# Hybrid decoder trunk: the activations become the loaded operand and the weights move past them, 512 columns a product; outputs by token, turned between stages

## The chip, the cores and the metric

The kernel runs on one core of a Trainium2 chip. It is judged by the device time of the whole program in microseconds, as the median of several runs. The engines spoken of are TensorE (PE in the rows, its loads of the stationary operand PEld), VectorE (DVE), ScalarE (ACT), GpSimd (POOL) and SyncE (SP), which issues the loads.

## The reference, cut to what matters

Two layers over 256 tokens of 1024 channels, all float32:

```python
for l in range(DEPTH):
    h = rms_norm(x, ffn1_norm[l])
    x = x + 0.5 * swiglu_ffn(h, ffn1_w_gate[l], ffn1_w_up[l], ffn1_w_down[l])   # 1024 -> 2816 -> 1024
    h = rms_norm(x, mix_norm[l])
    p = h @ w_in[l]                                                             # 1024 -> 2176
    a_val, a_gate, b_u, b_v, c_b, c_c, c_x = jnp.split(p, SPLITS, axis=-1)
    a = a_val * jax.nn.sigmoid(a_gate)
    a = causal_depthwise_conv(a, conv_a_w[l]) + conv_a_b[l]                     # width 31, 384 channels
    a = jax.nn.silu(layer_norm(a, ln_a_g[l], ln_a_b[l]))
    b = chunked_spatial_gating(jax.nn.gelu(b_u), jax.nn.gelu(b_v), ...)
    c = c_b * causal_depthwise_conv(c_c * c_x, conv_c_w[l])                     # width 3
    x = x + jnp.concatenate([a, b, c], axis=-1) @ w_out[l]
    h = rms_norm(x, ffn2_norm[l])
    x = x + 0.5 * swiglu_ffn(h, ffn2_w_gate[l], ffn2_w_up[l], ffn2_w_down[l])
return rms_norm(x, final_norm)
```

## The kernel before, in words

Everything lies by channel: x is eight tiles of 128 channels x 256 tokens. A weight matrix is cut in blocks of 128x128; a block is the stationary operand of TensorE and the 256 tokens move past it. The 2544 blocks of the whole program come from HBM in the order in which they are used, 8 blocks (512 KB) to a page, 318 pages.

Products are made in three parts. Each page is split in two fp32r pages, `hi` by a cast on ACT (L128) and `lo` = raw - hi on DVE (L129); activations are split in the same way and lie as hi|lo, 512 columns, side by side. `mm` (L170) makes a block's product with two matmuls: `wh` past all 512 columns (L175), then `wl` past the 256 hi columns (L176). So a finished bank holds two halves, and `whole` (L178) adds them with an ACT copy and a DVE add. Pages are split ahead of their use (`split_to`, `weights`, up to AHEAD = 14 pages); in the mixer `state["cap"]` stops that at the end of the mixer's own weights. A few products are made in plain float32 from the raw pages, one matmul call to a block that the chip runs as two instructions (`mm_native`, L149): the first 16 blocks of the program, and 40 blocks of each `w_out`.

A feed-forward part runs in two halves: gate and up projections of 11 column blocks, SiLU, split, then the down projection of that half, which is added to x. A norm's scale is a number per token, that is per column here: the squares are summed by small matmuls (`token_sums`, L270), the root is made on DVE (`rsqrt_rows`, L236), and the result is spread over the partitions by two small matmuls (L260).

The mixer's projections come in the order of `IN_ORDER`: group A first (gate and value of three channel blocks), then B, then C. As soon as a block of A has its gate and value, its convolution of 31 taps is queued in `back`: 16 products by ACT (L446, L449), the other 15 taps and the sums by DVE (L458, L451, L460, L461). `drain(BACK)` puts three of the queued steps behind each projection, and the rest after the last one. The mean of the layer norm over A (`m_la_mean`, L417) needs all three convolutions, and the products of `w_out` with A's channels come last in its order.

TensorE, DVE and ACT run their instructions in the order that the program's scheduler wrote, which follows the code above with small shifts; page splits of ACT and DVE stand in that same order.

Of the kernel before, what the change touches and what calls it, by code (L numbers as in the profile page):

```python
# [8 lines left out]
F32 = mybir.dt.float32  # L9
# [39 lines left out]
C_B = 2 * NA + 2 * NB
C_C, C_X = C_B + NC, C_B + 2 * NC  # L50
IN_ORDER = [t for i in range(NA) for t in (A_GATE + i, A_VAL + i)]
IN_ORDER += [B_V + i for i in range(NB)] + [B_U + i for i in range(NB)]
IN_ORDER += [t for i in range(NC) for t in (C_C + i, C_X + i, C_B + i)]

PAGE_BLOCKS = 8
PAGE = PAGE_BLOCKS * P
RAWS = 6
PARTS = 15
LOAD_AHEAD = 6
AHEAD = 14  # L60
PACE = 1.6
NEXT = 4
WORK = 12
EVAC = 6
WARM = 8
HALF = FT // 2
STEPS = 3
AFTER = 2
N_OPEN = 5
NATIVE_OUT = 5  # L70
WIDE = 16
BACK = 3
OUT = (2, 2, 2, 2)
# [3 lines left out]
def hybrid_trunk(ctx, tc, x_t, par, w_st, b_s, wts, out):  # L77
# [5 lines left out]
    work = ctx.enter_context(tc.tile_pool(name="work", bufs=WORK))  # L83
    tmp = ctx.enter_context(tc.tile_pool(name="tmp", bufs=2))
    ps_mm = ctx.enter_context(tc.tile_pool(name="ps_mm", bufs=6, space=PSUM))
    ps_sm = ctx.enter_context(tc.tile_pool(name="ps_sm", bufs=2, space=PSUM))

    spare = []

    def single(name):  # L90

        if not spare:
            pair = work.tile([P, 2, T], F32, tag="w", name=f"{name}_2")
            spare.extend([pair[:, 1, :], pair[:, 0, :]])
        return spare.pop()
# [15 lines left out]
    state = {"at": 0, "cap": None, "credit": 0.0}  # L111
# [20 lines left out]
    def native(n):  # L132

        at = state["at"]
        state["at"] += n
        last = (at + n - 1) // PAGE_BLOCKS
        load_to(last + LOAD_AHEAD)
        got = []
        for i in range(at, at + n):
            raw = loaded[i // PAGE_BLOCKS]  # L140
            c = i % PAGE_BLOCKS * P
            got.append(raw[:, c:c + P])
        while len(pages) <= last:
            pages.append(None)
        return got

    def mm_native(ps, w, act, ks, first, last):
        for k in ks:
            nc.tensor.matmul(ps, w[k], act[k], start=k == first, stop=k == last)  # L149

    def weights(n, ahead=True):
# [11 lines left out]
        got = []  # L163
        for i in range(at, at + n):
            hi, lo = pages[i // PAGE_BLOCKS]
            c = i % PAGE_BLOCKS * P
            got.append((hi[:, c:c + P], lo[:, c:c + P]))
        return got

    def mm(ps, w, act, ks, first, last):  # L170


        for k in ks:
# [4 lines left out]
    def whole(ps, name):  # L178

        if len(ps.shape) == 2:  # L180
            return ps
        lo = tmp.tile([P, T], F32, tag="e", bufs=EVAC, name=f"{name}_lo")
        nc.scalar.copy(lo, ps[:, 1, :])  # L183
        sm = tmp.tile([P, T], F32, tag="e", bufs=EVAC, name=f"{name}_sm")
        nc.vector.tensor_add(sm, ps[:, 0, :], lo)  # L185
        return sm
# [5 lines left out]
    ps = ps_sm.tile([P, P], F32, tag="sm", name="warm")  # L192
    for _ in range(WARM):
        nc.tensor.matmul(ps, ones_sq, ones_sq, start=True, stop=True)
    x_sb = acts.tile([P, DT, T], F32, tag="x", name="x_sb")
    x = [x_sb[:, d, :] for d in range(DT)]
    xall = x_t.rearrange("p (d t) -> p d t", t=T)
    par_sb = const.tile([P, NCOLS], F32, name="par_sb")
    nc.sync.dma_start(par_sb, par)
    for i in range(2):  # L200
        raw = raws.tile([P, PAGE], F32, tag="raw", name=f"raw{i}")
        loaded.append(raw)
    Q, H = DT // 4, PAGE // 2
    for n, (i, h) in enumerate(((0, 0), (1, 0), (0, 1), (1, 1))):
        nc.sync.dma_start(x_sb[:, n * Q:(n + 1) * Q, :], xall[:, n * Q:(n + 1) * Q, :])
        nc.sync.dma_start(loaded[i][:, h * H:(h + 1) * H], wts[i][:, h * H:(h + 1) * H])
# [5 lines left out]
    bsb = const.tile([P, NB, CHUNK], F32, name="bsb")  # L212

    apad = [const.tile([P, WA - 1 + T], F32, name=f"apad{i}") for i in range(NA)]
    zpad = [const.tile([P, WC - 1 + T], F32, name=f"zpad{i}") for i in range(NC)]
    for t, n in [(t, WA - 1) for t in apad] + [(t, WC - 1) for t in zpad]:
        nc.gpsimd.memset(t[:, :n], 0.0)

    def load_gating(l):
        nc.sync.dma_start(wst, w_st[l])  # L220
        nc.sync.dma_start(bsb, b_s[l])

# [5 lines left out]
    def col(l, name, i):  # L228
        c = (L * LCOLS if name == "final_norm" else l * LCOLS + COL[name]) + i
        return par_sb[:, c:c + 1]  # L230

    def pin(ins):
        return tc.keep_in_program_order(ins)


    def rsqrt_rows(ps, scale, eps, name, between=None):  # L236

        m = tmp.tile([P, 2], F32, tag="rs_m", name=f"{name}_m")
        nc.vector.tensor_scalar(m, ps, scale, eps, ALU.mult, ALU.add)
# [16 lines left out]
        if between is not None:  # L256
            between()
# [8 lines left out]
    def token_sums(tiles, name):  # L266
        ps = ps_sm.tile([P, 2], F32, tag="sm", name=f"{name}_ps")
        for h in range(2):
            for n, t in enumerate(tiles):
                pin(nc.tensor.matmul(  # L270
                    ps[:, h:h + 1], t[:, h * P:(h + 1) * P], ones,
                    start=n == 0, stop=n == len(tiles) - 1,
                ))
        return ps

    class Norm:


        def __init__(self, l, name):
            self.l, self.name, self.act = l, name, {}  # L280
            self.id = f"{name}{l}"
            self.sums = []
            self.first = False

        def begin(self):

            self.first, self.scaled = True, []
            for d in range(DT):
                xg = single(f"{self.id}_xg{d}")
                nc.vector.tensor_scalar(xg, x[d], col(self.l, self.name, d), None, ALU.mult)  # L290
                self.scaled.append(xg)
                x2 = acts.tile([P, 2, T], F32R, tag=f"x2{d}", name=f"{self.id}_x2{d}")
                nc.scalar.copy(x2[:, 0, :], xg)
                nc.vector.tensor_sub(x2[:, 1, :], xg, x2[:, 0, :])
                self.act[d] = x2

        def feed(self, d, split=True):
            if split:
                g = col(self.l, self.name, d)
                x2 = acts.tile([P, 2, T], F32R, tag=f"x2{d}", name=f"{self.id}_x2{d}")  # L300
                nc.scalar.activation(x2[:, 0, :], x[d], AF.Copy, scale=g)
                nc.vector.scalar_tensor_tensor(  # L302
                    x2[:, 1, :], x[d], g, x2[:, 0, :], ALU.mult, ALU.subtract)
                self.act[d] = x2
            self.square(d)
            if not split:
                nc.scalar.activation(x[d], x[d], AF.Copy, scale=col(self.l, self.name, d))
# [423 lines left out]
```

## Time and profile before

| | |
|---|---|
| time, median of 3 runs | 963.05 us (962.9 to 967.27) |
| the profiled execution | 961.55 us, its span 959.8 us |
| mean granted TensorE clock, share of full speed | 0.985 |
| busy share of the span: PE, DVE, ACT | 97%, 81%, 59% |

The span runs from the first to the last instruction that the profiler saw; 1.75 us of the profiled execution lie outside it. Times in rows are microseconds from the span's start.

### The profile page before, as it was taken

The numbers are of one execution on the slowest core, as the hardware profiler recorded it, in microseconds if no ns is written. First come the engines' busy times: TensorE is split into PE (matmuls) and PEld (weight loads), VectorE is DVE, ScalarE is ACT, GpSimd is POOL, SyncE is SP. The second block draws the span as 40 slices with busy tenths as digits, with TensorE's granted clock in tenths as the row PEclk, the third lists the DMA queues.
The fourth block names the chain that finished last, engine by engine and source line by source line (L and its number), as shares of the span: only waits on it lengthen the run. The fifth ranks groups of instructions, "written<-read, shape, count | busy, mean of one in ns | idle before, by whom it ended". The sixth has DMA issues, their size and how long they took to land.

```text
span 959.8 us, 14578 instructions
## 1 busy us (share of the span) xinstructions
PE 934.6 (97%) x5280; PEld 812.6 (85%) x5280; DVE 776.9 (81%) x1456; ACT 568.7 (59%) x1052; POOL 3.0 (0%) x14
## 2 busy tenths in 40 slices
PE   9999999999979999999999999999997999999995
PEld 7888888888868888888888888888886888888885
DVE  6998777878969997777987777778987799878733
ACT  6875555578257864555655545556952677645522
POOL 0000000000000000000000000000000000000000
PEclk9999999999979999999999999999998999999998
DMA  8995555530037975555555555554300789555101
GB/s 297 320 347 192 185 194 188 186 133 22 17 114 261 340 272 184 190 195 181 189 181 186 187 190 186 195 184 145 111 1 0 245 284 341 196 188 194 45 1 44
DMA packets 48024, 170.70 MB, mean 178 GB/s; under 512 B 5328, under 2 KB 5712, under 8 KB 47952
## 3 DMA queue, kind: packets, MB, share of 16 engines
q1 hardware_dynamic: 47952, 169.77, 50.8%
q8 instruction: 41, 0.67, 0.3%
q14 instruction: 31, 0.25, 0.1%
HBM read 168.71 MB, written 1.05 MB: 177 GB/s over the span
## 4 chain that ended last, share of the span: by engine, by line
PE 91%; DVE 6%; DMA 2%; ACT 1%; issue 0%; DVEq 0%; SPq 0%
PE f_pd L175 17%; PE f_pu L175 17%; PE f_pg L175 17%; PE f_pd L176 9%; PE f_pu L176 8%; PE f_pg L176 8%; PE m_p L175 7%; PE m_p L176 4%; PE m_po L149 1%; DMA raw<-wts 1%; DVE m_ac_acc L458 1%; DVE lo L129 1%; DVE m_ac_acc L451 1%; PE f_pg L149 1%; DMA x_sb<-x_t 0%
## 5 line engine op out<-in xcount | busy, mean ns | idle before, releaser
L129 DVE TENSOR_TENSOR lo<-raw,hi 128x1024 fp32r<-128x1024 f32 x306 | 371.8, 1222 | 95.3 <-ACT hi L128 93.8
L128 ACT CAST hi<-raw 128x1024 fp32r<-128x1024 f32 x306 | 318.8, 1051 | 212.8 <-PE f_pd L175 71.6
L175 PE MATMUL f_pg<-ffn_norm_x,hi 128*128 128x512 f32 x696 | 247.4, 395 | 1.7 <-DVE ffn_norm_x L302 1.7
L175 PE MATMUL f_pd<-f_m,hi 128*128 128x512 f32 x704 | 247.2, 396 | 0.0
L175 PE MATMUL f_pu<-ffn_norm_x,hi 128*128 128x512 f32 x696 | 247.0, 394 | 0.0
L176 PE MATMUL f_pd<-f_m,lo 128*128 128x256 f32 x704 | 195.5, 280 | 0.0
L176 PE MATMUL f_pg<-ffn_norm_x,lo 128*128 128x256 f32 x696 | 194.4, 279 | 0.0
L176 PE MATMUL f_pu<-ffn_norm_x,lo 128*128 128x256 f32 x696 | 194.3, 279 | 0.0
L175 PEld LDWEIGHTS f_pd<-f_m,hi 128*128 128x128 f32 x704 | 131.9, 188 | 32.1 <-DVE f_m L334 1.4
L175 PEld LDWEIGHTS f_pg<-ffn_norm_x,hi 128*128 128x128 f32 x696 | 130.5, 187 | 32.3 <-DVE ffn_norm_x L302 2.3
L175 PEld LDWEIGHTS f_pu<-ffn_norm_x,hi 128*128 128x128 f32 x696 | 130.5, 187 | 30.0
L176 PEld LDWEIGHTS f_pd<-f_m,lo 128*128 128x128 f32 x704 | 132.8, 189 | 0.5
L176 PEld LDWEIGHTS f_pg<-ffn_norm_x,lo 128*128 128x128 f32 x696 | 131.2, 188 | 0.3 <-DVE lo L129 0.3
L176 PEld LDWEIGHTS f_pu<-ffn_norm_x,lo 128*128 128x128 f32 x696 | 131.2, 188 | 0.1
L175 PE MATMUL m_p<-mix_norm_x,hi 128*128 128x512 f32 x304 | 108.1, 398 | 0.0
L176 PE MATMUL m_p<-mix_norm_x,lo 128*128 128x256 f32 x304 | 85.9, 283 | 0.0
L175 PEld LDWEIGHTS m_p<-mix_norm_x,hi 128*128 128x128 f32 x304 | 57.1, 188 | 12.9
L176 PEld LDWEIGHTS m_p<-mix_norm_x,lo 128*128 128x128 f32 x304 | 57.4, 189 | 0.4 <-issue 0.2
L389 ACT ACTIVATE f_sg<-f_g 128x256 f32<-128x256 f32 x88 | 36.4, 414 | 17.5 <-DVE f_g L387 17.3
L185 DVE TENSOR_TENSOR f_wd_sm<-f_pd,f_wd_lo 128x256 f32<-128x256 f32 x64 | 26.8, 419 | 20.6 <-ACT f_wd_lo L183 20.6
L333 ACT CAST f_m<-f_m 128x256 fp32r<-128x256 f32 x88 | 35.4, 402 | 10.5 <-DVE f_m L391 7.2
L458 DVE SCALAR_TENSOR_TENSOR m_ac_acc<-apad,par_sb,m_ac_acc 128x256 f32<-128x256 f32 x90 | 40.8, 481 | 0.8 <-ACT m_ac_acc L446 0.7
(242 smaller groups left out, 843.2 us busy)
## 6 DMA issues: line engine op xcount, KB each, us to landing
raw<-wts SPq DMA_DIRECT2D x316, 512.0 KB, 4.3
x_sb<-x_t SPq DMA_DIRECT2D x4, 256.0 KB, 5.2
raw<-wts SPq DMA_DIRECT2D x4, 256.0 KB, 5.4
out<-x_sb SPq DMA_DIRECT2D x4, 256.0 KB, 2.4
wst<-w_st SPq DMA_DIRECT2D x2, 256.0 KB, 4.3
bsb<-b_s SPq DMA_DIRECT2D x2, 128.0 KB, 4.2
par_sb<-par SPq DMA_DIRECT2D x1, 143.0 KB, 2.3
```

Of the source, the lines that this page charges most:

```text
L128: nc.scalar.copy(hi, loaded[i])
L129: after(nc.vector.tensor_sub(lo, loaded[i], hi), held[0])
L149: nc.tensor.matmul(ps, w[k], act[k], start=k == first, stop=k == last)
L175: nc.tensor.matmul(ps, wh, x2, start=k == first, stop=False)
L176: nc.tensor.matmul(ps[:, 0, :], wl, x2[:, 0, :], start=False, stop=k == last)
L185: nc.vector.tensor_add(sm, ps[:, 0, :], lo)
L333: nc.scalar.copy(x2[:, 0, :], src)
L389: nc.scalar.activation(sg, g, AF.Silu)
L451: nc.vector.tensor_add(acc, acc, t)
L458: yield lambda j=j: nc.vector.scalar_tensor_tensor(acc[:, j % 4, :], ap[:, j:j + T], wt[j], acc[:, j % 4, :], ALU.mult, ALU.add)
```

## The change

The operands of TensorE change places. An activation tile of 128 channels x 128 tokens is loaded (`xh` or `xl`), and 512 columns of a weight page move past it, so an output has 128 tokens on the partitions and 512 channels along the bank. `mm` makes three matmuls for a pair of operands, xh·wh, xh·wl and xl·wh, all into one bank; `whole` is gone, and so are the plain float32 products. All matmuls of `mm` go through the helper `matmul` (L92 in the listings below) and keep the program's order. Norm scales are now a number per partition, which ACT and DVE take as an operand: the small matmuls of `token_sums` and `rsqrt_rows` are gone but for the layer norm over A, and the squares are summed by ACT as it makes them.

Because the next product needs channels on the partitions again, the results are turned by TensorE: m in the feed-forward parts, x after each stage, group A's, B's and C's values in the mixer (`transposes`, 300 of 128x128 in the program; before there were 8). Per feed-forward group of 256 m channels two are made for each half of the tokens.

The down projection of a feed-forward part stays open in four banks (two token halves x two column halves) through all 11 groups. The mixer makes five groups of products of 512 columns (the last 384); the conv steps are queued when the second token half of A has been turned (`end_a`, which waits in `norm.later` for the first products of the next group), and are drained three at a time in groups 1 to 4, the rest after the first two k of `w_out`. The cap on splitting ahead is gone. x is loaded twice, by channel for the first norm (`begin`) and by token; whole pages are loaded between the quarters of x. RAWS and LOAD_AHEAD go from 6 to 4; a page holds 128 channels x 1024 weights, and w_in now takes 20 pages, 4 of them part padding.

```diff
-RAWS = 6
+RAWS = 4
-LOAD_AHEAD = 6
+LOAD_AHEAD = 4
...
-        while len(pages) < min(n, n_pages if state["cap"] is None else state["cap"]):
+        while len(pages) < min(n, n_pages):
...
-    def mm(ps, w, act, ks, first, last):
-        for k in ks:
-            (wh, wl), x2 = w[k], act[k]
-            nc.tensor.matmul(ps, wh, x2, start=k == first, stop=False)
-            nc.tensor.matmul(ps[:, 0, :], wl, x2[:, 0, :], start=False, stop=k == last)
+    def mm(ps, xs, ws, first, last):
+        (xh, xl), (wh, wl) = xs, ws
+        matmul(ps, xh, wh, start=first, stop=False)
+        matmul(ps, xh, wl, start=False, stop=False)
+        matmul(ps, xl, wh, start=False, stop=last)
...
-        pb = ps_sm.tile([P, T], F32, tag="sm", name=f"{name}_pb")
-        for h in range(2):
-            pin(nc.tensor.matmul(
-                pb[:, h * P:(h + 1) * P], y[:, h:h + 1].broadcast_to([P, P]), ident,
-                start=True, stop=True,
-            ))
-        return pb
+        return y
...
         def begin(self):
...
+                    nc.scalar.activation(hi, s, AF.Copy, scale=g)
+                    nc.vector.scalar_tensor_tensor(lo, s, g, hi, ALU.mult, ALU.subtract)
...
+        def turn(self, c, h):
+            hi, lo = self.tiles(c, h)
...
+            transposes([pt[:, d, :] for d in range(4)],
+                       [x[c, h][:, d * P:(d + 1) * P] for d in range(4)])
...
+            nc.vector.tensor_mul(xg, pt, g.broadcast_to([P, 4, P]))
+            nc.scalar.copy(hi, xg)
+            nc.vector.tensor_sub(lo, xg, hi)
...
+        for n, (c, h) in enumerate(banks):
+            ps = bank(c, h)
...
+            if n and not end:
+                nxt.turn(*banks[n - 1])
+            done(c, h, ps)
+        nxt.rstd()
+        if not end:
+            nxt.later.append(lambda: nxt.turn(*banks[-1]))
...
+        for c in range(TC):
+            for k in range(DT):
+                mm(got[c], norm.x2(k, c), ws[k], k == 0, k == DT - 1)
+            while norm.later:
+                norm.later.pop(0)()
+            yield got[c]
...
+            elif g < FG - 1:
+                wd[g - 1] = weights(GW)
+                for j in range(GW):
+                    for b in banks:
+                        down(g - 1, j, *b)
+                    if j == 0:
+                        turn(g, 1, ms[g, 1])
...
+        norm.later.append(lambda: end_a(0, 0, 2, av[1]))
...
+        for c, ps in groups(1, N):
...
+            a2[c] = glu(2, 1, r(c), ps[:, :128], ps[:, 128:256], c)
...
             drain(BACK)
...
+        norm.later.append(lambda: end_a(1, 2, 1, a2[1]))
...
+        for n, k in enumerate(OUT_ORDER[:NB]):
+            for b in banks:
+                outp(k, *b)
...
+        drain(len(back))
+        chain = layer_norm_a(l, conv, nm)
+        for k in OUT_ORDER[NB:NB + NC]:
+            for b in banks:
+                outp(k, *b)
+                next(chain, None)
```

The order of TensorE's instructions in the gate and up projections before; `f_8_pg` is the bank of a block's gate projection, `hi` and `lo` are pages.

```order
L175 MATMUL f_8_pg<-ffn_norm_x_148,hi_542 128x512
L176 MATMUL f_8_pg<-ffn_norm_x_148,lo_543 128x256
L175 MATMUL f_8_pg<-ffn_norm_x_153,hi_542 128x512
L176 MATMUL f_8_pg<-ffn_norm_x_153,lo_543 128x256
L175 MATMUL f_8_pg<-ffn_norm_x_157,hi_542 128x512
L176 MATMUL f_8_pg<-ffn_norm_x_157,lo_543 128x256
```

And now, at the end of the gate and up products of group 3 of the first feed-forward part; `f_pd` are the four open banks of the down projection, `f_mh` and `f_ml` the two parts of the turned m of the group before, `f_mt` the bank in which m is turned.

```order
L92 MATMUL f_3_p_639<-lo_480,ffn_norm_xh_136 128x512
L92 MATMUL f_3_p_639<-hi_479,ffn_norm_xl_137 128x512
L223 MATMUL f_mt_692<-ident,f_m_666 128x128 x2
L92 MATMUL f_pd_171<-hi_550,f_mh_580 128x512
L92 MATMUL f_pd_171<-lo_551,f_mh_580 128x512
L92 MATMUL f_pd_171<-hi_550,f_ml_581 128x512
L92 MATMUL f_pd_172<-hi_550,f_mh_580 128x512
L92 MATMUL f_pd_172<-lo_551,f_mh_580 128x512
L92 MATMUL f_pd_172<-hi_550,f_ml_581 128x512
```

The alternation of 512 and 256 columns has become a row of 512s, with two turns ahead of the down products and two more in their middle.

The order of DVE in the mixer's first layer before, where the last of the three convolutions ends; `m_ac_acc` is the sum over taps, `m_cr`, `m_cwb` and `m_co` belong to group C.

```order
L451 TENSOR_TENSOR m_ac_acc<-m_ac_acc,m_ac_t_3018 128x1024
L556 SCALAR_TENSOR_TENSOR m_bo_2_2966<-zpad_117,par_sb,m_bo_2_2966 128x256
L458 SCALAR_TENSOR_TENSOR m_ac_acc<-apad_114,par_sb,m_ac_acc 128x256
L556 SCALAR_TENSOR_TENSOR m_bo_2_2966<-zpad_117,par_sb,m_bo_2_2966 128x256
L458 SCALAR_TENSOR_TENSOR m_ac_acc<-apad_114,par_sb,m_ac_acc 128x256
L558 TENSOR_TENSOR m_cr_2982<-m_bo_2_2966,mix_norm_rb_2400 128x256
L458 SCALAR_TENSOR_TENSOR m_ac_acc<-apad_114,par_sb,m_ac_acc 128x256
L185 TENSOR_TENSOR m_cwb_sm<-m_p_2984,m_cwb_lo 128x256
L458 SCALAR_TENSOR_TENSOR m_ac_acc<-apad_114,par_sb,m_ac_acc 128x256
L561 TENSOR_TENSOR m_co_2_3009<-m_cwb_sm,m_cr_2982 128x256
```

And now, in the same mixer between the end of the second convolution and the end of the third; L126 is the page split on DVE, L418 the tap, L411 the sum of ACT's products.

```order
L126 TENSOR_TENSOR lo_2238<-raw_2124,hi_2237 128x1024
L126 TENSOR_TENSOR lo_2244<-raw_2130,hi_2243 128x1024
L126 TENSOR_TENSOR lo_2250<-raw_2229,hi_2249 128x1024
L525 SCALAR_TENSOR_TENSOR m_cv<-zpad,par_sb,m_cv 128x256 x2
L418 SCALAR_TENSOR_TENSOR m_ac_acc<-apad,par_sb,m_ac_acc 128x256
L525 SCALAR_TENSOR_TENSOR m_cv<-zpad,par_sb,m_cv 128x256
L418 SCALAR_TENSOR_TENSOR m_ac_acc<-apad,par_sb,m_ac_acc 128x256
L126 TENSOR_TENSOR lo_2341<-raw_2235,hi_2340 128x1024
L586 TENSOR_TENSOR m_cv<-m_ct_2347,m_cv 128x3x128
L586 TENSOR_TENSOR m_cv<-m_ct_2352,m_cv 128x3x128
L418 SCALAR_TENSOR_TENSOR m_ac_acc<-apad,par_sb,m_ac_acc 128x256
L126 TENSOR_TENSOR lo_2373<-raw_2241,hi_2372 128x1024
```

Page splits for later weights, which stood behind the convolutions, stand between their taps: 14 of them from the first tap of the mixer to the last, where the rows of the profile count 2 and 3 before.

The order of ACT in the same mixer now, from the group 1 products to the first product of the convolution (L406); L442 is the sigmoid of group A, L471 the copy of the turned values into the padded tile, L486 the GELU of group B.

```order
L442 ACTIVATE m_as_1922<-m_g_p_1891,mix_norm_y_1761 128x128
L471 COPY apad<-m_at_1857 128x2x256
L486 ACT_TABLE_LOAD
L486 ACTIVATE m_v_1926,m_sv<-m_g_p_1891,mix_norm_y_1761 128x256
L125 CAST hi_1875<-raw_1780 128x1024
L125 CAST hi_1881<-raw_1786 128x1024
L125 CAST hi_1887<-raw_1867 128x1024
L442 ACT_TABLE_LOAD
L442 ACTIVATE m_as_1960<-m_g_p_1892,mix_norm_y_1761 128x128
L406 ACTIVATE m_ac_acc<-apad,par_sb 128x256
L409 ACTIVATE m_ac_acc<-apad,par_sb 128x256 x3
```

Before, the first product of the convolution stood behind the sigmoid of the first channel block alone; now a sigmoid on the second token half of group 1 (`m_g_p_1892`, ended by TensorE's 96th product of the mixer) stands ahead of it.

## Rows read from the trace of the kernel before

**Rows 1.** The page: span, and busy time by engine with instructions.

```profile
span 959.8 us, 14578 instructions
PE 934.6 (97%) x5280; PEld 812.6 (85%) x5280; DVE 776.9 (81%) x1456; ACT 568.7 (59%) x1052; POOL 3.0 (0%) x14
```

**Rows 2.** Windows at the two mixers' layer norms: length, busy time, granted clock, DMA.

```profile
253.00:284.00 31.00, 25.96 (x108) 21.20 (x106) 24.45 (x64) 12.12 (x26) 1.25 (x1) 0.83 0.18 60
721.00:752.00 31.00, 24.39 (x104) 20.27 (x103) 23.52 (x61) 11.40 (x25) 0.00 (x0) 0.83 0.12 40
```

**Rows 3.** Timeline of PE, feed-forward parts: start, duration, instruction.

```profile
326.95 0.39 PE L175 MATMUL f_pg<-ffn_norm_x,hi 128*128 128x512 f32 x1
...
332.50 0.39 PE L175 MATMUL f_pg<-ffn_norm_x,hi 128*128 128x512 f32 x1
...
500.95 0.40 PE L175 MATMUL f_pg<-ffn_norm_x,hi 128*128 128x512 f32 x1
501.18 0.28 PE L176 MATMUL f_pg<-ffn_norm_x,lo 128*128 128x256 f32 x1
...
506.60 0.40 PE L175 MATMUL f_pg<-ffn_norm_x,hi 128*128 128x512 f32 x1
```

**Rows 4.** Timeline of PE, the float32 products and what follows them.

```profile
5.77 3.99 PE L149 MATMUL f_pg<-ffn_norm_xg,raw 128*128 128x256 f32 x8 [0.88 <-DVE ffn_norm_xg L290]
...
14.87 0.58 PE L175 MATMUL f_pg<-ffn_norm_x,hi 128*128 128x512 f32 x1
...
254.19 0.59 PE L149 MATMUL m_po<-m_vt,raw 128*128 128x256 f32 x2
254.62 0.59 PE L149 MATMUL m_po<-m_bo,raw 128*128 128x256 f32 x2
...
274.05 9.59 PE L149 MATMUL m_po<-m_ao,raw 128*128 128x256 f32 x30 [1.15 <-ACT m_ao L621]
283.29 0.58 PE L175 MATMUL m_po<-m_mix,hi 128*128 128x512 f32 x1
```

**Rows 5.** Timeline of PE, three transposes amid products of the second mixer.

```profile
716.67 0.28 PE L176 MATMUL m_p<-mix_norm_x,lo 128*128 128x256 f32 x1
716.79 0.49 PE L584 MATMUL m_pt<-ident,m_by 128*128 128x128 f32 x3
...
717.35 0.28 PE L176 MATMUL m_p<-mix_norm_x,lo 128*128 128x256 f32 x1
```

**Rows 6.** The chain of waits, small matmuls of the norms: start, duration.

```profile
200.53 0.34 PE mix_norm_ps L270 x4
...
226.81 0.43 PE m_lv_mean L417 x2
...
236.00 0.79 PE m_lv_ps L270 x8
...
245.25 0.44 PE m_lv_pb L260 x4
```

**Rows 7.** Timelines of DVE and ACT at the program's start.

```profile
7.28 0.62 DVE L290 TENSOR_SCALAR ffn_norm_xg<-x_sb,par_sb 128x256 f32<-128x256 f32 x2 [1.56 <-DMA x_sb<-x_t]
...
14.29 2.93 ACT L128 CAST hi<-raw 128x1024 fp32r<-128x1024 f32 x3
```

**Rows 8.** The mixer: instructions by tile and line, groups of DVE, the chain.

```profile
L175 PE MATMUL m_p<-mix_norm_x,hi x304: 391/395/581, 194.7 to 720.4; 128*128 128x512 f32 x152
...
L446 ACT ACTIVATE m_ac_acc<-apad,par_sb x6: 600/602/607, 208.6 to 697.1; 128x256 f32<-128x256 f32 x6
...
L458 DVE SCALAR_TENSOR_TENSOR m_ac_acc<-apad,par_sb,m_ac_acc 128x256 f32<-128x256 f32 x45 | 20.6, 486 | 0.4 <-ACT m_ac_acc L446 0.4
L451 DVE TENSOR_TENSOR m_ac_acc<-m_ac_acc,m_ac_t 128x1024 f32<-128x1024 f32 x9 | 11.0, 1218 | 0.1
L129 DVE TENSOR_TENSOR lo<-raw,hi 128x1024 fp32r<-128x1024 f32 x2 | 2.4, 1220 | 0.5 <-ACT hi L128 0.5
...
266.27 0.71 PE m_la_mean L417 x2
```

More of the change, by code (lines that the diff above doesn't have):

```diff
@@ L178, in whole @@
[L178 to L186, printed above, removed]
+        return pages[at:at + n]
+    def mm(ps, xs, ws, first, last):
[3 more added lines that the diff above has]
+        matmul(ps, xl, wh, start=False, stop=last)
@@ L198, in hybrid_trunk @@
     par_sb = const.tile([P, NCOLS], F32, name="par_sb")
     nc.sync.dma_start(par_sb, par)
[L200 to L206, printed above, removed]
+    xt = [parts.tile([P, 4, T], F32, tag="pg", name=f"xt{i}") for i in range(2)]
@@ L285, in begin @@
         def begin(self):
-            self.first, self.scaled = True, []
+            for c, h in banks:
+                self.tiles(c, h)
             for d in range(DT):
[L289 to L295, printed above, removed]
@@ L439, in conv_ops @@
+    def conv_ops(l, i, out, name):
+        ap = apad[:, i, :]
+        wt = [col(l, "conv_a_w", i * WA + j) for j in range(WA)]
         acc = parts.tile([P, 4, T], F32, tag="pg", name=f"{name}_acc")
@@ new lines, in turn, with groups, r @@
+        def turn(store, key, c, src, n, name):
+            if c == 0:
+                store[key] = ps_t.tile([P, n, T], F32, tag="t", name=f"{nm}_{name}t{key}")
+            transposes([store[key][:, j, c * P:(c + 1) * P] for j in range(n)],
+                       [src[:, j * P:(j + 1) * P] for j in range(n)])
+            return store[key]
+        def groups(i, width, ahead=True):
+            return enumerate(project(norm, weights(4, ahead), width, f"{nm}_g{i}"))
+        def r(c):
+            return norm.rs[:, c:c + 1]
@@ new lines, in mixer, with end_a @@
+        av = {}
+        for c, ps in groups(0, N):
+            if c:
+                turn(a_ps, 0, 0, av[0], 2, "a")
+            av[c] = glu(0, 2, r(c), ps[:, :256], ps[:, 256:], c)
+        def end_a(key, i, n, src):
+            pt = turn(a_ps, key, 1, src, n, "a")
+            nc.scalar.copy(apad[:, i:i + n, HA:], pt)
+            for t in range(i, i + n):
+                back.extend(conv_ops(l, t, conv[t], f"{nm}_ac{t}"))
+        norm.later.append(lambda: end_a(0, 0, 2, av[1]))
+        a2, vs = {}, {}
@@ new lines, in mixer, with end_z @@
+        cv = single("cv", NC)
+        def end_z(key, i, n, src):
+            pt = turn(z_ps, key, 1, src, n, "z")
+            nc.scalar.copy(zpad[:, i:i + n, HC:], pt)
+            for t in range(i, i + n):
+                wt = [col(l, "conv_c_w", t * WC + j) for j in range(WC)]
+                nc.scalar.activation(cv[:, t, :], zpad[:, t, 0:T], AF.Copy, scale=wt[0])
+                for j in range(1, WC):
+                    nc.vector.scalar_tensor_tensor(
+                        cv[:, t, :], zpad[:, t, j:j + T], wt[j], cv[:, t, :], ALU.mult, ALU.add)
@@ new lines, in mixer, with spatial @@
+        z0 = {}
+        for c, ps in groups(2, N):
+            if c:
+                turn(z_ps, 0, 0, z0[0], 1, "z")
+            us[c] = mx.tile([P, DB], F32, tag=f"u{c}", name=f"{nm}_u{c}")
+            nc.scalar.activation(us[c], ps[:, :DB], AF.Gelu_apprx_tanh, scale=r(c))
+            z0[c] = gate_c(ps, DB, 1, 0, c)
+            drain(BACK)
+        norm.later.append(lambda: end_z(0, 0, 1, z0[1]))
+        def spatial(c):
+            pz = ps_t.tile([P, DB], F32, tag="t", name=f"{nm}_pz{c}")
+            for h in range(HB):
+                matmul(pz[:, h * 64:(h + 1) * 64], wst[:, h, :], vs[c][:, h * 64:(h + 1) * 64],
+                       start=True, stop=True)
+            b = tmp.tile([P, DB], F32, tag="b", name=f"{nm}_b{c}")
+            nc.vector.tensor_tensor(
+                b.rearrange("p (h e) -> p h e", h=HB), pz.rearrange("p (h e) -> p h e", h=HB),
+                bsb.rearrange("p (h o) -> p h o", o=1).broadcast_to([P, HB, 64]), op=ALU.add)
+            nc.vector.tensor_mul(b, b, us[c])
+            return b
@@ new lines, in mixer, with end_b @@
+        bs = {}
+        z1 = {}
+        for c, ps in groups(3, N):
+            if c:
+                turn(z_ps, 1, 0, z1[0], 2, "z")
+            z1[c] = gate_c(ps, 0, 2, 1, c)
+            bs[c] = spatial(c)
+            drain(BACK)
+        def end_b():
+            store = {}
+            for c in range(TC):
+                pt = turn(store, 0, c, bs[c], NB, "b")
+            hi, lo = (mids.tile([P, NB, T], F32R, tag="mid", name=f"{nm}_b{p}") for p in "hl")
+            nc.scalar.copy(hi, pt)
+            nc.vector.tensor_sub(lo, pt, hi)
+            for i in range(NB):
+                mix[NA + i] = (hi[:, i, :], lo[:, i, :])
@@ new lines, in mixer, with end_c @@
+        norm.later.append(lambda: end_z(1, 1, 2, z1[1]))
+        norm.later.append(end_b)
+        cb = {}
+        for c, ps in groups(4, DC):
+            cb[c] = tmp.tile([P, DC], F32, tag="cb", name=f"{nm}_cb{c}")
+            nc.scalar.activation(cb[c], ps, AF.Copy, scale=r(c))
+            drain(BACK)
+        def end_c():
+            o = cv
+            for c in range(TC):
+                pt = ps_t.tile([P, NC, P], F32, tag="t", name=f"{nm}_ct{c}")
+                transposes([pt[:, j, :] for j in range(NC)],
+                           [cb[c][:, j * P:(j + 1) * P] for j in range(NC)])
+                t = slice(c * P, (c + 1) * P)
+                nc.vector.tensor_mul(o[:, :, t], pt, cv[:, :, t])
+            hi, lo = single("ch", NC, F32R), single("cl", NC, F32R)
+            nc.scalar.copy(hi, o)
+            nc.vector.tensor_sub(lo, o, hi)
+            for i in range(NC):
+                mix[NA + NB + i] = (hi[:, i, :], lo[:, i, :])
@@ L675, in _channels @@
+    for c, h in banks:
+        y = tmp.tile([P, N], F32, tag="sq", name=f"y{c}{h}")
+        nc.vector.scalar_tensor_tensor(
+            y, x[c, h], norm.rs[:, c:c + 1], gfin[0][:, h * N:(h + 1) * N], ALU.mult, ALU.mult)
+        nc.sync.dma_start(out[c, :, h * N:(h + 1) * N], y)
 def _channels(a):
```

710 lines of the change are left out of this document (299 added, 411 removed).

## The prediction

> **What bounds the kernel now.** I read the page first: TensorE is busy for 934.6 of 959.8 us, DVE for 81% and ACT for 59% [rows 1]. So the time is TensorE's stream of instructions plus its few gaps. The question is then what a unit of that stream costs, where the gaps are, and whether the new kernel makes either larger.
>
> What a unit costs must be read from the distance between starts, since a record lasts longer than the distance to the next one. Sixteen block products take 500.95 to 506.60, 0.3531 us each, and in another place 326.95 to 332.50, 0.3469 [rows 3]. I take the mean, 0.350. In such a pair the next start comes 0.23 after the 512 columns and 0.12 after the 256 [rows 3]: the cost is proportional to columns, 0.350 for 768, so 0.2333 for 512.
>
> The gaps lie in the two mixers, around the layer norm over A. In two windows of 31 us PE is busy for 25.96 and 24.39, so it idles for 5.04 + 6.61 = 11.65 us, and the granted clock falls to 0.83 [rows 2]. Where do they come from? The first product of group A's convolution starts on ACT at 208.6, 13.9 us after the mixer's first product at 194.7; the mean that needs all three convolutions starts on PE at 266.27 [rows 8], 71.6 after the first product. That is nearly the moment at which TensorE gets there anyway. The convolution is just hidden, with little to spare. At DVE's own rate the 57.7 us from 208.6 to the mean hold 45 taps and 9 sums of 1.22 us, and only 2 page splits of 1.22 [rows 8].
>
> **The change part by part, in TensorE's time.**
>
> *Products.* A block of weights took 768 columns before (512 + 256) and takes 768 now: three products of 128 tokens for two token halves. 2544 blocks are 3744 matmuls of 512 columns and 96 of 384. At 0.2333 and, in proportion, 0.175 this is 873.5 + 16.8 = 890.3 us. Before, 2448 blocks went by pairs, 856.8 us, and 96 by float32. Those are the only ones that the change makes cheaper: the first 16 take 5.77 to 14.87, 9.1 us; two blocks are 0.43 apart per block while the clock is full (254.19 to 254.62, two instructions for one block), so 25 blocks of a w_out take 10.75; its last 15 take 274.05 to 283.29, 9.24, partly at the lower clock [rows 4]. With the second mixer taken as the first: 9.1 + 2 x 19.99 = 49.1. The sum before is 905.9, so this part gives **-15.6**. The bounds for the 512-column distance are 0.231 and 0.235 by the two places (-24 to -8); lower is rival 1.
>
> *Turns.* 292 more transposes. In the second mixer three of them lie in a pair's stretch: the next lo matmul starts at 717.35, 0.68 after the one at 716.67, where it would be 0.35; so 0.11 each [rows 5]. 292 x 0.11 = **+32**. They are made by the engine that sets the time and nothing hides them. The records of a transpose last longer than that distance, as those of all matmuls do. The Trainium skill ("TensorE: Matmul & The Clock Gate", Part 4) gives about 275 ns for a transpose in a kernel's context; by it the sum would have 80 here, +48 us. I take the distance, because it is what delays the next product.
>
> *Small matmuls that go.* Seven norms lose the sums and the spreading, 0.34 + 0.44 each (the spreading as for the layer norm, four matmuls), and each mixer loses the layer norm of v on TensorE, 2 x 0.43 + 0.79 + 0.44 [rows 6]: 5.5 + 4.2 = **-9.7**.
>
> *DVE and ACT in the feed-forward parts.* `whole`, one ACT copy and one DVE add for every bank, goes; a group makes larger but fewer steps. DVE has less to do, but TensorE never waited for it there, so I count nothing. Splits of pages remain 1.22 us of DVE and 0.98 of ACT [rows 7, 8] against 2.8 us of TensorE (8 blocks). Should the loads with RAWS = 4 run late, a gap would show there; 512 KB per 2.8 us is what the stream asked for before too. I count nothing.
>
> *Start.* The float32 products began on raw data at 5.77 [rows 4]. Now every product needs split pages. In the present kernel the second quarter of x is there at 7.28 [rows 7], behind half a page; behind a whole page I put it at 8.1. In the order on ACT all eight activations of the first two quarters stand ahead of the first page's cast: about 1.2 us for four, then the cast (2.93 / 3 = 0.98 [rows 7]) and the split on DVE, 1.2. The second product needs that lo: 11.5 us. So +5.7, and as the first matmuls run at the lower clock like the first ones now, **+7** (4 to 9).
>
> *Norms between stages.* Five times x is turned for the next product. The fourth bank's turn is put behind the first token half's products, and on DVE two page splits (2.4 us) stand ahead of its lo part; the products that need it come after 12 others, 2.8 us. Multiplying, casting and splitting a bank take about as long again. I put less than 1 us each, **+4** in all (0 to 7).
>
> *The mixers.* Let T be the mixer's first product. TensorE's walk to the mean: four groups of 48 matmuls, 4 x 11.2; group 4, 8.4; 22 turns, 2.4; ten banks of w_out, 3 x 0.2333 each, 7.0; together 62.6, and some 6 of waits on the way (group B's and C's split parts are made late, by ACT and DVE, just before they are used). TensorE is at the mean at about T + 69, much as now.
>
> The convolution is later at both ends. *Its beginning:* on ACT the first tap product stands behind the sigmoid on the second token half of group 1, which needs TensorE's 96th matmul, T + 22.4. Today the lag from three projections (24 blocks, 8.4) to the first tap is 13.9 - 8.4 = 5.5; with the same lag it starts at T + 28, 14 us later than now. *Its length:* 14 page splits stand between the first tap and the last on DVE, against 2; 12 x 1.22 = +14.6. What goes from the same stretch of DVE is the `whole` adds and multiplications by norm scales, some 20 steps of 0.42, about 8; and turning needs a few new ones. 57.7 + 14.6 - 10 = 62. So the last convolution is done at T + 90, and TensorE, with its order pinned, waits there for some 19 to 20 us. Behind it wait the rest of w_out, the next norm and everything after. The chain from the mean to A's products keeps its own waits, some 5. So about 24 per mixer. Bounds: 10 if the lag at the start is short and DVE squeezes its steps together, 35 if ACT, with 48 products and as many casts, holds DVE up as well. Two mixers: **+48 -11.65**. After such a wait TensorE restarts at the lower clock, as now behind the gap: 15 float32 blocks took 9.24 where 15 x 0.43 = 6.45 were due [rows 4]. That loss left with the float32 term and comes back: 2 x 2.8, **+5**.
>
> **Sum**, against the profiled execution: 959.8 - 15.6 + 32 - 9.7 + 7 + 4 + 48 - 11.65 + 5 = 1018.9 us of span; 1.75 lie outside it (961.55 in all), so 1020.6. The median of the runs shown, 963.05, is 1.5 above that execution; I say **1020**.
>
> **Rivals.**
>
> *1. A 512-column matmul behind a 512-column one starts at 0.216.* The float32 products, two instructions of 512 columns' worth to a block, start 0.43 / 2 = 0.215 apart [rows 4]; perhaps the 0.233 is the price of changing between 512 and 256. Against it: the 0.12 behind 256 columns is the same 9% over the bare columns, which looks like a price per column of fp32r. The Trainium skill (same page, "Back-to-back issue gap") has N / 2.4 + 2.5 ns, 216 ns. The gain would be 3744 x 0.0175 = 65, of which the mixers' longer waits take some 3: 1020 - 62 = 958, not slower than before. It decides from 0.2175 down: there all other terms (+59) are paid. Chance 0.16.
>
> *2. The convolution stays hidden.* Should the scheduled order run so that DVE is done when TensorE arrives, the mixers keep the gaps they have: 1020 - 48 + 11.65 - 5 = 979; were even these gone, 967. For it: DVE is freed from many steps, and page splits may be early. Against it: 57.7 us of DVE work now, beginning 14 us later, in the same 70. Chance 0.12.
>
> *3. Turns cost what their records last, about 0.27.* Each of the 300 would then hold the stream for a record rather than 0.11: +48, 1068. For it: two at a time between dependent products, unlike the three seen. Against it: all of those that the trace has, amid such products, cost 0.11. The sentence of the skill above is this case. Chance 0.07.
>
> *Forecast:* 0.65, itself 990 to 1045 (mixers -28 to +22, products and start another 10 either way).
>
> **How the numbers follow.** A run of this kernel can't tell less than about 0.5% from no change. Faster: most of rival 1 (0.12) and 0.02 of rival 2 with other terms small, 0.14. Same: 0.04 of rival 1 and 0.03 of rival 2, 0.07. Slower: the rest, 0.79. The range from 956 to 1045 leaves out the lower part of rival 1 (about 0.08), rival 3 (0.07) and the ends of the forecast.
>
> **What would show it.** Right: starts of successive 512s 0.233 apart in the feed-forward parts; 0.11 per turn, 0.22 for two; the first real product at 11 to 12 us; one gap of 15 to 25 us per mixer ended by DVE's last convolution step, T + 85 to T + 95, with a clock below 1 behind it. Wrong: 0.216 between starts makes it rival 1 at once; a convolution done by T + 70, rival 2; a product delayed by 0.5 behind two turns, rival 3. A wait in the feed-forward parts, for loads or for m's turned parts, is in none of the cases and would add to all.

## The result, and the profile after

The changed kernel takes 1025.03 us (median of 4 runs, 1023.81 to 1027.33) against 963.35 before: a ratio of 1.0633, 95% interval 1.0598 to 1.0669. Predicted were 1020 and slower.

The page of the kernel after, against [rows 1]: the instruction counts fell, TensorE's idle time grew from 25 to 81 us.

```profile
span 1022.3 us, 11571 instructions
PE 941.4 (92%) x4232; PEld 767.6 (75%) x4232; DVE 612.4 (60%) x868; ACT 510.6 (50%) x732; POOL 2.1 (0%) x10
```

TensorE's waits in the whole program: what waited, for whom, us in total, times, longest.

```profile
PE m_mean L92 <- DVE m_ac L421: 39.9, 4, 10.7
PE m_zt L223 <- DVE m_cz L513: 6.3, 4, 2.0
PE f_p L92 <- ACT hi L125: 5.8, 1, 5.8
PE f_mt L223 <- DVE f_m L365: 3.0, 3, 2.2
PE m_g_p L92 <- DVE mix_norm_xl L269: 2.8, 2, 1.4
PE f_p L92 <- DVE ffn_norm_xl L269: 2.6, 3, 1.4
```

Half of the idle time is one wait, twice: the mean of group A's layer norm waits for the convolution, 20 us in each mixer. Its first instance on PE's timeline:

```profile
280.22 0.59 PE L92 MATMUL m_mean<-m_ac,ones_sq 128*128 128x256 f32 x2
290.04 1.22 PE L92 MATMUL m_mean<-m_ac,ones_sq 128*128 128x256 f32 x2 [9.22 <-DVE m_ac L421]
302.01 1.22 PE L92 MATMUL m_mean<-m_ac,ones_sq 128*128 128x256 f32 x2 [10.75 <-DVE m_ac L421]
```

The mixer's first product is at 206.0, so TensorE arrives at T + 74 and the last convolution is there at T + 96. From the first product of a stage to that of the next, the mixers take 119.0 us each (97.3 and 97.0 before), the two feed-forward parts between them 379.3 (371.1), the first 195.3 (188.9); the first product comes 4.9 us later. These are +43.8, +8.2, +6.3 and +4.9; the last part is 0.7 shorter: +62.5 in all, the difference of the spans.

The gate and up products on PE's timeline, and the turns behind them, against [rows 3] and [rows 5]:

```profile
439.64 0.39 PE L92 MATMUL f_p<-hi,ffn_norm_xh 128*128 128x512 f32 x1
...
450.29 0.39 PE L92 MATMUL f_p<-hi,ffn_norm_xl 128*128 128x512 f32 x1
450.52 0.38 PE L223 MATMUL f_mt<-ident,f_m 128*128 128x128 f32 x2
450.66 0.48 PE L92 MATMUL f_pd<-hi,f_mh 128*128 128x512 f32 x1
450.97 0.40 PE L92 MATMUL f_pd<-lo,f_mh 128*128 128x512 f32 x1
```

47 distances from 439.64 to 450.29 are 0.2266 each, not 0.2333. From 450.29 to 450.97 lie two products and two turns: 0.68 - 0.46 = 0.22, 0.11 a turn.

### The profile page after: what moved, and what is told of

Same layout as the page of the kernel before. It is cut to its first block, busy times and chain, and to the rows that moved or that the text cites. A ratio compares the mean times of both kernels' runs of the same rounds, so it can differ in the third digit from the quotient of the medians.

```text
span 1022.3 us, 11571 instructions
## 1 busy us (share of the span) xinstructions
PE 941.4 (92%) x4232; PEld 767.6 (75%) x4232; DVE 612.4 (60%) x868; ACT 510.6 (50%) x732; POOL 2.1 (0%) x10
## 4 chain that ended last, share of the span: by engine, by line
PE 79%; DVE 11%; ACT 5%; DMA 3%; issue 1%; SPq 0%; DVEq 0%; ACTq 0%
PE f_p L92 43%; PE f_pd L92 23%; PE m_g_p L92 6%; DVE lo L126 4%; PE m_po L92 3%; DVE m_ac_acc L418 2%; DMA raw<-wts 2%; PE f_mt L223 2%; ACT hi L125 2%; DVE m_ac_acc L411 2%; ACT m_ac_t L409 1%; DMA xt<-x_t 1%; PE m_pz L92 1%; PE ffn_norm_pt L223 0%; ACT ffn_norm_xh L252 0%
## 5 line engine op out<-in xcount | busy, mean ns | idle before, releaser
L126 DVE TENSOR_TENSOR lo<-raw,hi 128x1024 fp32r<-128x1024 f32 x320 | 390.1, 1225 | 159.9 <-ACT hi L125 130.2
L92 PE MATMUL f_p<-hi,ffn_norm_xh 128*128 128x512 f32 x704 | 276.5, 393 | 5.9 <-ACT hi L125 5.8
L92 PE MATMUL f_p<-hi,ffn_norm_xl 128*128 128x512 f32 x704 | 275.4, 391 | 2.6 <-DVE ffn_norm_xl L269 2.6
L92 PE MATMUL f_p<-lo,ffn_norm_xh 128*128 128x512 f32 x704 | 274.8, 390 | 0.5 <-DVE lo L126 0.5
L92 PEld LDWEIGHTS f_p<-hi,ffn_norm_xh 128*128 128x128 f32 x704 | 132.6, 188 | 34.0 <-ACT hi L125 6.1
L92 PEld LDWEIGHTS f_p<-hi,ffn_norm_xl 128*128 128x128 f32 x704 | 132.6, 188 | 32.4 <-DVE ffn_norm_xl L269 4.7
L92 PEld LDWEIGHTS f_p<-lo,ffn_norm_xh 128*128 128x128 f32 x704 | 132.6, 188 | 28.2 <-DVE lo L126 1.0
L92 PE MATMUL f_pd<-hi,f_mh 128*128 128x512 f32 x352 | 146.1, 415 | 0.0
L92 PE MATMUL f_pd<-hi,f_ml 128*128 128x512 f32 x352 | 139.5, 396 | 1.3 <-DVE f_ml L340 1.3
L92 PE MATMUL f_pd<-lo,f_mh 128*128 128x512 f32 x352 | 138.2, 393 | 0.0
L92 PEld LDWEIGHTS f_pd<-hi,f_ml 128*128 128x128 f32 x352 | 66.4, 189 | 17.8 <-DVE f_ml L340 2.6
L92 PEld LDWEIGHTS f_pd<-lo,f_mh 128*128 128x128 f32 x352 | 66.8, 190 | 11.8
L92 PEld LDWEIGHTS f_pd<-hi,f_mh 128*128 128x128 f32 x352 | 66.6, 189 | 11.1
L92 PE MATMUL m_g_p<-hi,mix_norm_xl 128*128 128x512 f32 (+1 forms) x160 | 62.8, 393 | 2.8 <-DVE mix_norm_xl L269 2.8
L92 PE MATMUL m_g_p<-hi,mix_norm_xh 128*128 128x512 f32 (+1 forms) x160 | 64.4, 403 | 0.0
L92 PE MATMUL m_g_p<-lo,mix_norm_xh 128*128 128x512 f32 (+1 forms) x160 | 62.5, 391 | 0.0
L92 PE MATMUL m_mean<-m_ac,ones_sq 128*128 128x256 f32 x12 | 6.1, 601 | 39.9 <-DVE m_ac L421 39.9
L418 DVE SCALAR_TENSOR_TENSOR m_ac_acc<-apad,par_sb,m_ac_acc 128x256 f32<-128x256 f32 x90 | 39.1, 480 | 0.7
L92 PEld LDWEIGHTS m_g_p<-hi,mix_norm_xl 128*128 128x128 f32 x160 | 31.4, 197 | 8.8 <-DVE mix_norm_xl L269 3.6
```

Of the source, the lines that this page charges most:

```text
L92: return pin(nc.tensor.matmul(*a, **k))
L418: yield lambda j=j: nc.vector.scalar_tensor_tensor(acc[:, j % 4, :], ap[:, j:j + T], wt[j], acc[:, j % 4, :], ALU.mult, ALU.add)
```

## The experiments

Theory A is the prediction's: the convolution begins late, and page splits among its taps lengthen DVE's work. Theory B came with the trace of after: only one of the three convolutions was done when TensorE stood waiting. The groups of DVE from 273.3 to 302 show the other two (line, shape, count, busy, mean ns):

```profile
L418 DVE SCALAR_TENSOR_TENSOR m_ac_acc<-apad,par_sb,m_ac_acc 128x256 f32<-128x256 f32 x30 | 12.8, 480 | 0.2
L411 DVE TENSOR_TENSOR m_ac_acc<-m_ac_acc,m_ac_t 128x1024 f32<-128x1024 f32 x6 | 7.4, 1226 | 1.9 <-ACT m_ac_t L409 1.4
L126 DVE TENSOR_TENSOR lo<-raw,hi 128x1024 fp32r<-128x1024 f32 x2 | 2.4, 1216 | 0.0
```

30 of 45 taps and 6 of 9 sums stand there, behind nearly everything else. B says that the ration of three steps a drain put them there: the mixer now has eight drains where it had one behind nearly every of 17 projections.

**Drains of eight steps** (E1).

```diff
-BACK = 3
+BACK = 8
```

> BACK = 8 instead of 3: eight convolution steps are queued behind each projection half, nothing else. In the changed kernel DVE and ACT had done only one of the three convolutions when TensorE stood at the mean; of DVE's 60 convolution instructions of a mixer 37 stand behind group C's last split part, now 2. The number of page splits between the first and the last tap is 13 instead of 14. Theory A (the prediction: the convolution begins late and page splits lengthen it, so its work does not fit): the wait at the mean stays within 16 to 20 us per mixer, time 1017 to 1025. Theory B (the queue's ration of three steps leaves two convolutions for the end, while DVE idles before): DVE's idle time of about 9 us between the first tap and the mean is filled, the wait falls to 8 to 12 us per mixer, time 1000 to 1010.

Measured: 1012.52 us, -12.5, between both. The wait at the mean is gone, but TensorE's time is taken by others: those for group C's turned values grew from 6.3 to 12.8, and one for group B's appears.

```profile
PE m_zt L223 <- DVE m_cz L513: 12.8, 4, 5.5
PE m_po L92 <- DVE m_bl L566: 9.1, 2, 4.5
```

So the wait moved ahead with the steps. The mixers became 6.5 and 7.5 us shorter, most of it idle time of DVE that was filled. From the first tap to the mean, in after and in E1 (length, then busy time of PE, PEld, DVE, ACT), DVE is busy for 60.24 of 69.66 us and for 58.67 of 62.30:

```profile
232.34:302.00 69.66, 45.23 (x205) 37.48 (x203) 60.24 (x111) 44.93 (x87) 0.64 (x1) 0.83 0.40 130
```

```profile
234.20:296.50 62.30, 46.22 (x203) 38.23 (x202) 58.67 (x112) 43.89 (x87) 1.20 (x1) 0.87 0.42 137
```

**The cap on splitting ahead, alone** (E2). It is set at the mixer's start, and `split_to` stops there.

```diff
+        state["cap"] = state["at"] + 28
...
         mix.update(next(chain))
+        state["cap"] = None
```

> Page splitting stops at the end of the mixer's own 28 pages until its convolutions are done; 6 page splits instead of 14 stand between the first and the last tap, the drains stay as they were (30 of the 60 convolution instructions still behind C's last split part). Theory A: 8 splits of 1.22 us less, so the wait at the mean falls by about 10 us per mixer, time near 1005. Theory B: DVE idles where the splits stood, the wait falls by what 7 steps take, 3 to 5 us per mixer, time 1014 to 1019. Both: the splits put off must be caught up in the next feed-forward part; a wait for pages there would take the gain back.

Measured: 1000.14 us, -24.9: A's direction, and more than A said; B's range is missed by far. The mixers take 101.6 and 104.2, 17.4 and 14.8 less than in after. The wait at the mean gives 8 of that (24.3 us left in the program). In the first mixer TensorE also comes to the mean at T + 67 and not T + 74: it waits less on the way, and its granted clock stays at 1.00 from 238 to 266.3, where after has 0.90 from 238 to 270.7.

**Both** (E3).

> The cap and BACK = 8 together. Theory A: as the cap alone, near 1005. Theory B: both add up, the convolution ends when TensorE arrives, the wait at the mean is below 4 us per mixer, time 985 to 993.

Measured: 988.20 us, -36.8; the two effects add (12.5 + 24.9 = 37.4). The first mixer of after, of E1, E2 and E3, each from its first product to the next stage's: length, then busy time of PE, PEld, DVE, ACT.

```profile
206.00:325.00 119.00, 91.38 (x415) 74.19 (x413) 92.53 (x175) 74.25 (x132) 0.64 (x1) 0.89 0.41 133
```

```profile
207.80:320.30 112.50, 92.15 (x415) 74.68 (x413) 90.59 (x175) 73.13 (x132) 1.20 (x1) 0.92 0.43 141
```

```profile
206.90:308.60 101.70, 86.68 (x416) 71.57 (x414) 82.28 (x167) 65.73 (x124) 1.13 (x1) 0.93 0.35 114
```

```profile
206.00:303.50 97.50, 87.15 (x414) 71.68 (x413) 81.50 (x167) 65.27 (x124) 1.57 (x1) 0.96 0.37 119
```

From after to E2 the cap takes 10 us of DVE's work out of the mixer (8 splits); the drains take out idle time. What E3 leaves is as long as the mixer before. And its first tap still starts at T + 26, as in after:

```profile
L406 ACT ACTIVATE m_ac_acc<-apad,par_sb x6: 586/592/598, 232.4 to 744.2; 128x256 f32<-128x256 f32 x6
```

**DVE's time put back without the pages** (E12, E3 with empty work), because the cap also freed page slots and ACT.

```diff
+            for _ in range(3 if n == BACK else 0):
+                after(nc.vector.tensor_sub(dummy, x_sb[:, 0, :T], x_sb[:, 1, :T]), last)
```

> The cap with BACK = 8 and, behind each of its eight drains in a mixer, three subtractions of 128x256 on DVE whose result nobody reads: about as much DVE time as the 8 page splits that the cap took out of the mixer (24 of 0.42 us at most, 8 to 10 us), but no cast on ACT, no page slot and no load. If the cap helped by DVE's time alone, the mixers get about 8 to 10 us longer each and the time is 1002 to 1008. If it helped by free page slots, by ACT's casts or by loads, the time stays within 988 to 993.

Measured: 1003.73 us, +15.5 on E3, and the mixers 7.8 and 8.1 longer, as expected if DVE's time counts by itself. The added group on DVE, and the first mixer (DVE busy for 89.50 us, 81.50 in E3):

```profile
L432 DVE TENSOR_TENSOR m_dummy<-x_sb 128x256 f32<-128x256 f32 x24 | 10.0, 417 | 0.1
```

```profile
206.30:311.60 105.30, 88.34 (x415) 72.72 (x413) 89.50 (x191) 65.36 (x124) 1.70 (x1) 0.95 0.33 110
```

But this is not all that the cap gave. From E1 to E3, which differ by the cap alone, the mixers became 15.0 and 13.7 us shorter and the program 24.3. DVE's time put back brings some 8 of these 14 to 15 us. About 3.4 of the rest lie behind the mean, where no empty work was put: from the last product of the mean to the next stage it takes 22.5 us in E1, 19.1 in E3 and in E12. Whether ACT's casts, page slots or the loads make the rest, no run shows.

**An earlier turn** (E5, on the changed kernel).

```diff
-        norm.later.append(lambda: end_a(0, 0, 2, av[1]))
+        end_a(0, 0, 2, av[1])
```

> The second half of group A's first two blocks is turned right behind group 0's products and not behind the first half of group 1, so that the convolution can begin some 5 us sooner; TensorE may wait 2 us there. Drains (3) and splitting as in the changed kernel. If the late beginning by itself costs time (the step of the prediction: 14 us late, each us of it paid at the mean), the wait at the mean falls by 3 to 5 us per mixer: 1016 to 1021. If the queue's ration of three steps decides, the later steps stay where they were and the time stays within 1023 to 1028.

Measured: 1030.58 us, +5.5; both expectations missed. The padded tile is filled 14 us before the first tap reads it, but the tap stands behind the sigmoid in ACT's order, and that became later with TensorE's products: the tap is at T + 30.6, where after has T + 26.4. The first line is after's, the others are E5's:

```profile
232.34 0.59 ACT L406 ACTIVATE m_ac_acc<-apad,par_sb 128x256 f32<-128x256 f32 x1
```

```profile
223.80 0.59 ACT L471 COPY apad<-m_at 128x512 f32<-128x512 f32 x1 [1.81 <-PE m_at L223]
...
237.70 0.37 ACT L442 ACTIVATE m_as<-m_g_p,mix_norm_y 128x128 f32<-128x128 f32 x1
237.97 0.59 ACT L406 ACTIVATE m_ac_acc<-apad,par_sb 128x256 f32<-128x256 f32 x1
```

So the run tested a later beginning, not an earlier one. The convolution begins 4.2 us later and ends at T + 97.1 instead of T + 96.0, 1.1 later; the wait at the mean is what it was:

```profile
PE m_mean L92 <- DVE m_ac L421: 39.9, 4, 10.7
```

The time went mostly to TensorE's new wait for the turn (4.7 us in all). That a late beginning costs little by itself, E3 and this run show.

**Every turn twice** (E4).

```diff
             pin(nc.tensor.transpose(d, s, ident))
+            pin(nc.tensor.transpose(d, s, ident))
```

> Every turn is made twice (600 transposes instead of 300, same result). If a turn holds the stream for the 0.11 us between starts, +33 us less what falls into waits that are there anyway (44 of the turns lie in the mixers): 1050 to 1058. If it costs its record of about 0.27 us: +81, above 1095. If turns were hidden beside the other matmuls: no change.

Measured: 1056.93 us, +31.9 for 300 turns, 0.106 each. Four in a row on PE's timeline start 0.11 apart, with records of 0.27:

```profile
465.85 0.27 PE L223 MATMUL f_mt<-ident,f_m 128*128 128x128 f32 x1
465.95 0.27 PE L224 MATMUL f_mt<-ident,f_m 128*128 128x128 f32 x1
466.06 0.27 PE L223 MATMUL f_mt<-ident,f_m 128*128 128x128 f32 x1
466.17 0.27 PE L224 MATMUL f_mt<-ident,f_m 128*128 128x128 f32 x1
```

Rival 3 is out.

**Equal matmuls in the old arrangement** (E9, one run).

```diff
-            nc.tensor.matmul(ps[:, 0, :], wl, x2[:, 0, :], start=False, stop=k == last)
+            nc.tensor.matmul(ps, wl, x2, start=False, stop=k == last)
```

> The kernel before, with the second matmul of each pair made as wide as the first (the low weight part past all 512 columns; 256 columns of work more per block, which only adds the product of the two low parts). It asks what a 512-column matmul behind a 512-column one costs there. If the price is 0.2333 as in the prediction's sum: a pair takes 0.467 and the time is about 1250. If a row of equal matmuls settles at the 0.227 that the changed kernel shows in its gate and up products: 0.453, about 1217. If 0.216 (rival 1): 0.432, about 1165.

Measured: 1193.91 us, below the middle expectation, because the longer stream hides the mixers' gaps: no wait in them is left in TensorE's list, and they grew by 8.3 and 8.6 us, where 176 pairs at 0.103 more each would be 18. The distance is the middle one: 32 from 499.63 to 506.88, 0.2266.

```profile
499.63 0.39 PE L175 MATMUL f_pu<-ffn_norm_x,hi 128*128 128x512 f32 x1
499.86 0.39 PE L176 MATMUL f_pu<-ffn_norm_x,lo 128*128 128x512 f32 x1
...
506.88 0.39 PE L175 MATMUL f_pu<-ffn_norm_x,hi 128*128 128x512 f32 x1
```

**The start** (E8): the first page's split behind the first quarter of x, the next ones behind the others, in `begin`.

```diff
+                if d % 2:
+                    split_to(d // 2 + 1)
```

> On ACT and DVE the first page's split stands behind the first quarter of x, not behind the second; the others follow in turn. Nothing else. If the eight activations ahead of the cast hold the first product (the prediction's step), it starts 1 to 2.5 us sooner than at 10.7 and the time falls by as much: 1022 to 1024. If the page's arrival holds it, no change.

Measured: 1020.44 us; the first product starts at 8.81 instead of 10.69, so the eight activations held it. The runs of both kernels lie from 1020.2 to 1027.3, and the two profiled spans differ by 1.0; the gain is between 1 and 5. The same edit on E3 (E11, below) gives 4.6 by the medians.

**Towards a better version.** Six steps a drain with the cap (E6):

> The cap with BACK = 6 instead of 8: fewer convolution steps stand ahead of group C's steps on DVE. If the waits for group C's products (7.8 us of TensorE with BACK = 8) come from convolution steps queued ahead of them, they fall by about 4 us in all, against a wait at the mean that grows by 2 to 6: 984 to 992, no clear gain. If steps are simply better spread, below 984.

Measured: 996.13 us, worse than either expectation: group C's waits fell from 7.8 to 4.7, that at the mean grew from 2.8 to 10.9. All four edits together (E7):

> The cap lifted as soon as the convolutions' steps are queued, BACK = 6, the earlier turn, and the first page cast behind the first quarter of x. Sum of the single expectations: 988 less 2 to 3 at the start, less 3 to 8 of waits for m's steps in the feed-forward parts: 975 to 984. It should stay above 963, since some 30 us of turns are left against some 10 us that steadier products give back.

Measured: 1000.06 us, a miss by 16; it holds E5's wait and E6's. The cap lifted earlier, with eight steps and the new start (E10):

> The cap with BACK = 8, the first page's split behind the first quarter of x, and the cap lifted as soon as all convolution steps are queued. If the single effects add: 988 less 2 to 4 at the start, less 3 to 6 of TensorE's waits for m's steps in the feed-forward parts after a mixer: 979 to 984. Not below 975, since nothing of the turns (32 us) is touched.

Measured: 991.55 us, a miss: the waits for m fell from 9.0 to 3.0, but the mixers took 103.6 and 104.1. Page splits come back among the layer norm's steps: 8 stand behind the last convolution step in each mixer where E11 has 4, and from the mean to the next stage it takes 23.6 and 23.9 us where E11 takes 19.1. Without that edit (E11):

> The cap with BACK = 8 (988.2) and the first page's split behind the first quarter of x, nothing else. The two effects should add: 984 to 986.

Measured: 983.57 us, the best of these and 1.021 (1.018 to 1.0239) of before. Its mixers take 97.6 and 98.1 (97.3 and 97.0 in the kernel before); what is left over lies in the feed-forward parts, where the turns are (+15.8), and at the start (+2.6).

## Why the prediction was right, step by step

The time was right to 0.5%, and that is in part luck: the products were put some 14 us too dear, the two mixers together some 14 us too cheap.

*Products.* The term was mis-sized. I took 0.2333 from pairs of 512 and 256 columns. In the gate and up products, steady rows of 512s, it is 0.2266, below the bounds that I gave (0.231 to 0.235); in the down products, with turns between, about 0.231. Over 2112 gate and up products 0.0067 each is 14 us less than the sum had. The feed-forward parts between the mixers grew by 8.2 us, where my terms (120 turns, two norms) gave 13. Rival 1 was right that a row of equal matmuls is cheaper (E9), and wrong in the size: 0.2266, not 0.216. The Trainium skill ("TensorE: Matmul & The Clock Gate", "Back-to-back issue gap") gives the 216 ns of that rival for an isolated matmul of 512 columns, and about 131 ns in a stream of loads and matmuls; the rows here agree with neither.

*Turns.* Right, by place and by size: 0.11 on the timeline, 0.106 by E4. The records of 0.27 overlap with what follows. The Trainium skill's 275 ns for a transpose ("TensorE: Matmul & The Clock Gate", Part 4) agrees with the record and not with the price.

*Start.* Right: the first page's cast and split held the first products (10.69, 11.95; I had 11.5 for the second); the stages begin 4.9 us later, and the first matmuls run slower besides. E8 shows the cause.

*Norms.* TensorE waited 2.8 + 2.6 = 5.4 us for the lo parts; +4 was said, 0 to 7 as bounds.

*The mixers.* The wait at the mean was right, 20 us each, with 19 to 20 forecast; so were its release by DVE's last convolution step, and the splits as a main cause (E2, and for about half of their effect E12). But both ends of the wait came 5 to 6 us later than forecast, TensorE at T + 74 (T + 69) and the convolution at T + 96 (T + 90, and outside the T + 85 to T + 95 that was to show it). That they cancelled is luck. The first mixer of after in stretches; the first three lead up to the mean, the fourth is the wait (length, busy time of PE, PEld, DVE, ACT, POOL, granted clock, DMA):

```profile
206.00:238.00 32.00, 30.62 (x140) 24.83 (x139) 20.77 (x39) 23.23 (x37) 0.00 (x0) 1.00 0.55 181
238.00:270.70 32.70, 29.55 (x141) 26.07 (x140) 29.00 (x57) 20.78 (x38) 0.64 (x1) 0.90 0.50 162
270.70:280.20 9.50, 8.18 (x37) 6.07 (x37) 9.39 (x14) 7.15 (x13) 0.00 (x0) 1.00 0.77 245
280.20:302.70 22.50, 2.53 (x8) 1.29 (x6) 20.34 (x38) 11.37 (x25) 0.00 (x0) 0.60 0.04 13
302.70:325.00 22.30, 20.50 (x97) 15.94 (x95) 13.02 (x31) 11.72 (x22) 0.00 (x0) 0.94 0.28 95
```

Two things in the step on the convolution failed. First, the late beginning: it came as forecast (T + 26.4, T + 28 said), and I paid 14 us for it; but in E3 the first tap is as late and the wait is down to 1.4 per mixer, and in E5 4.2 us of lateness cost 1.1. Second, I took DVE as busy throughout. Its work was sized rightly, 60 us of 62 said, but it idled for 9.4 us between the first tap and the mean, because the drains gave it too few steps; E1 and E3 show 4 to 7.5 us per mixer for that.

The whole mixer grew by 21.9 us, where my terms (float32 products out, turns in, small matmuls out, wait, clock) give about 15. The excess is not idle time: TensorE idles for 5.9 us on the way to the mean (6 said) and for 1.8 behind it (5 said). Without waits its walk took 68.4 us instead of 62.6. My sum for it leaves out the matmuls of group B's gating and has no stretch at the lower clock, while the second stretch above shows a mean granted clock of 0.90. No run separated these.

Rival 2 fell for this kernel, but E3 shows that it could be had with two edits.

## What to carry to other kernels

When products change shape, count the calls of whatever is rationed per call: the same "three steps behind each projection" left two thirds of the work for the end. And check an engine with 60% of the whole program busy stage by stage: here DVE, freed by a fifth overall, set the length of the two mixers, and 8 page splits for a later stage cost at least their full time there (17.4 and 14.8 us for 10 us of splits, E2). A turn made by the engine that sets the time must be paid at its distance between starts, times its count, before anything is won by the other layout.

## What the runs showed of the hardware that was not expected

A row of equal 512-column fp32r products starts every 0.2266 us in the gate and up products of both arrangements (47 distances in the changed kernel, 32 in E9), whichever operand is loaded; 512 and 256 columns in turn cost 0.2313 or 0.2354 per 512 columns [rows 3]. E9 shows that the difference of 2 to 4% goes with the alternation of widths. Why the down products of the changed kernel, 512s too, stand at about 0.231, no run shows.
